# Two groups of experts at 128 slots with split weights, two at 64 slots with raw fp32 weights in column halves

## The chip, the cores and the metric

The kernel runs on one core of a Trainium2 chip. The metric is the device time of one execution in microseconds (us); the median of several executions is compared.

Names of engines in all that follows: PE is TensorE (matmuls), DVE is VectorE, ACT is ScalarE, POOL is GpSimd, SP is SyncE, which here issues the transfers of weights. A piece is one transfer of weights from HBM into on-chip memory; here it is 1 MB (1024 KB, 1.0486 million bytes).

## What is computed

Two layers of a transformer block over 256 tokens and 256 context tokens of width 1024: four kinds of attention, a gated merge, and a mixture of experts. The last layer keeps only the 256 tokens. The change touches the mixture of experts of that last layer:

```python
def moe(tok, router_w, router_b, w1, w3, w2):          # tok: 256 x 1024 in the last layer
    scores = jax.nn.sigmoid(tok @ router_w)            # 16 experts in 4 groups of 4
    biased = scores + router_b
    group = argmax(sum of the 2 best of biased in each group)   # one group per token
    idx = the 2 best experts of that group
    wts = scores[idx] / sum(scores[idx])
    ...
    y_e = (silu(x @ w1[e]) * (x @ w3[e])) @ w2[e]      # w1, w3: 1024 x 512, w2: 512 x 1024
    out[token] = sum over its 2 experts of wts * y_e
```

All weights are fp32. Every one of the 16 experts is used by some token, so all 16 x 6 MB are read.

## The kernel before

TensorE's fast path here multiplies a reduced fp32 type (fp32r). To keep fp32 accuracy the kernel splits every operand into an exact high and low part and forms a product by three matmuls (`mm3`, L262: high x high, high x low, low x high; they are the rows L263, L264 and L265).

The last layer's experts. Each token chooses one group of four experts. The routing (L1543 to L1660) computes on chip, on small tables, which group a token takes and its rank in the group; group g owns the 128 slots from 128 g on, so 512 slots in all. A one-hot matrix `OH` [token, slot] (L1620) gathers the tokens into the slots by matmuls (L1633); the gathered tokens are scaled (`hf`, L1637), and split into the parts `xe`, which share the buffer `hT` (L1640, L1641). `group_tables` (L1706) gathers the weights of a slot (`wsl`) and the transposed one-hots `OHT`.

The loop over experts (L1731) goes through them in the order 0 to 15. Step i forms x @ w1 and x @ w3 of expert i (two times 8 x 3 matmuls of 128x512 into the banks `h1` and `h3`), `act_in` makes silu times product times slot weight, and then, for expert i - 1, four transposes (L258) and 4 x 2 x 3 matmuls with w2 into two banks that collect the four experts of a group. After a group's last expert the sum is split (`y_parts`, L1467) and goes back to the tokens by matmuls with `OHT` (`combine`, L1480, L1486), which adds to the residual `xt` (L1495). At step 1 `overflow` (L1499) reads the largest count of a group (`mxi`, a number in a register of every engine), and a branch (L1504) runs a second, general pass over all experts for tokens beyond the 128 slots.

The weights. The class `Stream` (L93) holds the pieces in the order of use. `issue` (L117) starts transfers from SP while fewer than `cap` buffers are in use (7 for the experts, set at L1728); a transfer is one row L131. `_split` (L137) makes the parts: ACT copies to the high part `whi` (L285), DVE subtracts to get the low part `wlo` (L289), each sixth time POOL instead (L287). A raw buffer is free when all of its 512-column quarters are split. Four pairs of `whi` and `wlo` exist. The order of everything on an engine is that in which the program issues it, as rearranged by the framework's scheduler.

What waits for what around the change: SP issues a piece when its buffer is free, so it stands behind the splits; ACT and DVE stand behind the landing of a piece and behind PE (a pair of parts must be used before it is overwritten); PE stands behind the splits.

Of the kernel before, what the change touches and what calls it, by code (L numbers as in the profile page):

```python
# [19 lines left out]
P = 128  # L20
# [3 lines left out]
NE = 16  # L24
# [9 lines left out]
# packed small parameters: name -> width  # L34
# [5 lines left out]
for _n, _w in SM:  # L40
# [4 lines left out]
# packed constants (shapes alone)  # L45
CS = [("ident", 128), ("natm", 64), ("cos", 64), ("sin", 64), ("cosm", 32), ("sinm", 32),
      ("iota", 128), ("encg", 4), ("pidx", 1), ("cv", 32), ("one", 1), ("sel", 32)]
# [8 lines left out]
def shape_constants():  # L56
# [23 lines left out]
    put("iota", j)  # L80
    put("encg", 4.0 - np.arange(4)[None, :])
# [11 lines left out]
class Stream:  # L93
    """Weights in the order of use: DMA ahead, then exact high and low parts ahead of TensorE."""
# [19 lines left out]
    def issue(self):  # L114
        while self.nd < min(len(self.pieces), self.lim) and (self.live < self.cap or self.spare):
# [11 lines left out]
            for (p0, p1, s) in pc["loads"]:  # L127
# [45 lines left out]

    def done(self, i):
        self.live -= 1


SP2, SP4, SPT = 1, 1, 1
ADA_ORDER = ((1, 0), (0, 1), (0, 2), (1, 1), (1, 2))
# [8 lines left out]
def kernel(ctx: ExitStack, tc: tile.TileContext, a, out, dbg=None, depth=L):  # L188
# [65 lines left out]
    def transposes(src, kts):  # L254
        """Transposes of 128-column blocks of src into one bank."""
# [5 lines left out]
    def mm3(o, s, whl, start, stop):  # L261
        """s = (high, low) stationary parts, whl = (high, low) moving parts."""  # L262
# [13 lines left out]
    # silu(c), silu(c_ctx): row k = p * KT + kt of ada_w  # L276
# [32 lines left out]
    def plan_ada0():  # L309
        """The first modulation by columns: scale and shift of two blocks of d at a time."""  # L310
# [5 lines left out]
    def plan_in0():  # L316
        """Keys, values and queries of the window heads by rows, as h comes first."""
# [36 lines left out]
    def plan_out(l):  # L354
        """w_out by halves of its columns, for one pair of tiles of tokens after the other."""
# [23 lines left out]

    for l in range(depth):  # L380
# [14 lines left out]
        plan_out(l)  # L395
        for i in range(NE + 1):
# [53 lines left out]
    def ada_bias(l, r):  # L450
        """ada_b, and for the last round the second norm's gain, laid out as the products."""
# [41 lines left out]
    # biases of the first modulation (shift, scale) and the first norms' gains, d on partitions  # L493
# [12 lines left out]
    def ada0(c):  # L506
        """Scale and shift of blocks 2c and 2c + 1 of d; four column groups hold parts of the sum."""
# [92 lines left out]
    def rope_tables(T):  # L600
        """Gains times the rotations' cosines and sines; the router's tables share their place."""
# [19 lines left out]
    def attention_layer(l, T, hT):  # L621
# [24 lines left out]
        def norm_heads(x, H, hd, ct, stt, rot0):  # L646
            """x [P, H, hd] in SBUF, in place: rms over hd, gain and rotation."""
# [35 lines left out]
        def qk_post(nats, tiles, H, gname, dst, lo=None):  # L683
# [6 lines left out]
            def p2(t):  # L690
# [5 lines left out]
                else:  # L696
                    # of each head the high part on its own rows, the low part on those of the other
# [36 lines left out]
        def std_slots(operands, vsel, yT, pairs, sink=False, bias=None, mask=False):  # L734
            """Slots of work: P V of one pair of heads, scores of the next unit, transposes of the one before."""
# [114 lines left out]
        def heads(q, k):  # L850
            """Products of a pair of heads: the high part of the queries with both parts of the keys, then the low one."""
# [10 lines left out]
        def stage_win():  # L862
# [14 lines left out]
            def kv(t):  # L877
                """By tiles of tokens: h comes so from the layer before."""
# [246 lines left out]
    def steps0(ev_kv, ev_q):  # L1125
        """The first projections, block by block of d as the modulation arrives."""
# [39 lines left out]
    for l in range(depth):  # L1166
# [10 lines left out]
        def run_ada(steps, stage):  # L1177
            """With the rounds of the modulation that go with this stage."""
# [65 lines left out]
        wm.lim = E_IDS[l, NE - 1, 2][-1][-1][0] + 1  # L1244
# [34 lines left out]
        # router weights with the second norm's gain, and what its shift adds to the logits  # L1279
# [15 lines left out]
        def finish(t, j, ps):  # L1295
            """Half of the columns of a tile of x; its part of the logits."""
# [74 lines left out]
        if nT > 2:  # L1371
            norms()
        if not last:
# [543 lines left out]
```

## Time and profile before

| | us |
|---|---|
| runs | 2021.88, 2022.29, 2023.82 |
| median | 2022.29 |
| the profiled execution: its span, and with what lies around it | 2020.5, about 2022.3 |
| last layer's experts, first to last matmul of their loop | 1711.8 to 2010.4 |

| engine | busy us | share of the span |
|---|---|---|
| PE | 1902.2 | 94% |
| DVE | 1456.5 | 72% |
| ACT | 1255.0 | 62% |
| POOL | 812.2 | 40% |

The span is the time from the first to the last instruction of the profiled execution; 1.8 us lie around it up to the median of the runs. A matmul of the fast type is one record in the timeline; a raw fp32 matmul of 256 or 512 columns is two, so x8 of such a row are four matmuls. "Granted clock" is the share of full speed that TensorE's throttle gave. "DMA share" is the mean busy share of the 16 transfer engines of the core.

### The profile page before, as it was taken

How to read it: one execution, taken by the hardware profiler on the slowest of the kernel's cores; microseconds unless marked ns; L12 is line 12 of the kernel's file. 1: busy time of each engine (PE TensorE's matmuls, PEld its weight loads, DVE VectorE, ACT ScalarE, POOL GpSimd, SP SyncE). 2: the span in 40 equal slices, each digit the busy share in tenths (PEclk: the TensorE clock that was granted, in tenths of full speed). 3: DMA queues.
4: the chain of work that ended last, by engine and by line, in shares of the span. 5: the costliest groups of instructions: out<-in, count | busy, mean ns of one | idle time of the engine just before them, and what ended most of it. 6: DMA issues, size and time to landing. Idle time of an engine off the chain costs nothing. (4 is left out here: it accounts for less than half of the span.)

```text
span 2020.5 us, 28368 instructions
## 1 busy us (share of the span) xinstructions
PE 1902.2 (94%) x9124; PEld 1412.6 (70%) x9124; DVE 1456.5 (72%) x2614; ACT 1255.0 (62%) x2605; POOL 812.2 (40%) x1126
## 2 busy tenths in 40 slices
PE   7989999999999999599999979999999998999998
PEld 5746678776666677377777766667777676777776
DVE  4657465657556546788888976865767776999998
ACT  4436465455435435389999855554656555889887
POOL 0657353536346400544433326641446511323231
PEclk9989999999999999699999988999999998999999
DMA  9340242211662347689999572355322473899995
GB/s 337 123 139 29 76 136 71 63 42 41 261 231 63 106 137 260 231 290 358 361 357 352 201 265 88 147 198 167 105 92 62 125 273 124 293 342 355 335 331 198
DMA packets 174145, 392.23 MB, mean 194 GB/s; under 512 B 13089, under 2 KB 30785, under 8 KB 168864
## 3 DMA queue, kind: packets, MB, share of 16 engines
q1 hardware_dynamic: 167200, 377.29, 53.9%
q0 software_dynamic: 4320, 7.94, 1.1%
q10 hardware_dynamic: 2464, 5.08, 0.7%
q8 instruction: 75, 1.23, 0.3%
q14 instruction: 86, 0.70, 0.1%
HBM read 381.21 MB, written 16.84 MB: 197 GB/s over the span
## 5 line engine op out<-in xcount | busy, mean ns | idle before, releaser
L285 ACT ACTIVATE whi<-raw 128x512 fp32r<-128x512 f32 x608 | 374.5, 631 | 61.9 <-PE h L265 34.8
L289 DVE TENSOR_TENSOR wlo<-raw,whi 128x512 fp32r<-128x512 f32 x509 | 378.1, 791 | 41.1 <-ACT whi L285 40.5
L251 ACT ACTIVATE whi<-raw 128x512 fp32r<-128x512 f32 (+1 forms) x376 | 231.7, 625 | 251.2 <-PE acc L265 188.3
L264 PE MATMUL acc<-wlo,hT 128*128 128x512 f32 (+2 forms) x976 | 385.0, 394 | 0.2 <-DVE wlo L252 0.2
L265 PE MATMUL acc<-whi,hT 128*128 128x512 f32 (+2 forms) x976 | 379.1, 390 | 0.2 <-DVE hT L252 0.2
L252 DVE TENSOR_TENSOR wlo<-raw,whi 128x512 fp32r<-128x512 f32 (+1 forms) x376 | 278.3, 751 | 136.1 <-ACT whi L251 134.8
L263 PE MATMUL acc<-whi,hT 128*128 128x512 f32 (+2 forms) x976 | 363.9, 398 | 2.9 <-ACT nat L955 1.1
L287 POOL TENSOR_TENSOR wlo<-raw,whi 128x512 fp32r<-128x512 f32 x99 | 140.0, 1414 | 295.4 <-ACT whi L285 270.9
L263 PEld LDWEIGHTS acc<-whi,hT 128*128 128x128 f32 x976 | 182.6, 189 | 55.7 <-issue 11.1
L264 PEld LDWEIGHTS acc<-wlo,hT 128*128 128x128 f32 x976 | 184.1, 189 | 44.2 <-issue 8.5
L265 PEld LDWEIGHTS acc<-whi,hT 128*128 128x128 f32 x976 | 183.8, 188 | 39.3 <-issue 5.8
L238 POOL TENSOR_SCALAR pp<-pp,sml 128x512 f32<-128x512 f32 (+1 forms) x168 | 119.4, 720 | 143.3 <-DVE sml L731 92.9
L726 ACT ACTIVATE pp<-S,sml 128x512 f32<-128x512 f32 (+1 forms) x192 | 117.2, 612 | 86.1 <-DVE sml L721 58.3
L721 DVE TENSOR_REDUCE sml<-S 128x1 f32<-128x512 f32 (+1 forms) x192 | 112.8, 596 | 43.7 <-PE S L712 42.2
L558 POOL TENSOR_TENSOR sml<-sml,nhalf 128x1 f32<-128x1 f32 (+3 forms) x110 | 121.2, 1104 | 7.0
L557 POOL TENSOR_SCALAR sml<-sml 128x1 f32<-128x1 f32 (+3 forms) x110 | 38.5, 350 | 191.1 <-DVE sml L652 114.2
L264 PE MATMUL h<-wlo,hT 128*128 128x512 f32 x256 | 105.0, 410 | 6.2 <-DVE wlo L289 5.8
L264 PE MATMUL h<-wlo,xe 128*128 128x512 f32 x256 | 105.5, 412 | 5.2 <-POOL wlo L287 4.0
L289 DVE TENSOR_TENSOR wlo<-w,whi 128x512 fp32r<-128x512 f32 x139 | 99.6, 760 | 11.7 <-ACT whi L285 11.7
L258 PE MATMUL T<-cst,pp 128*128 128x128 f32 x560 | 91.2, 286 | 12.9 <-POOL pp L238 9.3
L264 PE MATMUL S<-wlo,yh 128*128 128x512 f32 x256 | 103.1, 403 | 0.0
L285 ACT ACTIVATE whi<-w 128x512 fp32r<-128x512 f32 x160 | 96.8, 630 | 9.5 <-PE S L265 2.5
(383 smaller groups left out, 3900.8 us busy)
## 6 DMA issues: line engine op xcount, KB each, us to landing
raw<-in_moe_w_dram SPq DMA_DIRECT2D x152, 1024.0 KB
raw<-in_w_in_dram SPq DMA_DIRECT2D x124, 512.0 KB
raw<-in_ada_w_dram SPq DMA_DIRECT2D x48, 1024.0 KB
w<-in_moe_w_dram SPq DMA_DIRECT2D x16, 1024.0 KB
w<-in_moe_w_dram SPq DMA_DIRECT2D x64, 256.0 KB
raw<-in_w_branch_dram SPq DMA_DIRECT2D x24, 512.0 KB
raw<-in_w_out_dram SPq DMA_DIRECT2D x24, 512.0 KB
w<-in_moe_w_dram SPq DMA_DIRECT2D x16, 512.0 KB
```

The costliest lines, as they stand in the source:

```text
L238: G.tensor_scalar(o, i, s, s2, op0=OP.mult, op1=OP.mult)
L251: act(hi, src, AF.Copy)
L252: V.tensor_tensor(lo, src, hi, op=OP.subtract)
L263: mm(o, s[0], whl[0], start=start, stop=False)
L264: mm(o, s[0], whl[1], start=False, stop=False)
L265: mm(o, s[1], whl[0], start=False, stop=stop)
L285: act(hi, raw, AF.Copy)
L287: G.tensor_tensor(lo, raw, hi, op=OP.subtract)
L289: V.tensor_tensor(lo, raw, hi, op=OP.subtract)
L558: G.tensor_tensor(r, r, nhalf[:, :n], op=OP.pow)
L721: V.tensor_reduce(nm[:, i:i + 1], ps[i][:, :nk], axis=AX.X, op=OP.max, negate=True)
L726: act(p[:, :nk], ps[i][:, :nk], AF.Exp, bias=nm[:, i:i + 1], accum_out=nm[:, 2 + i:3 + i])
```

## The change

The diff does six things in the last layer.

1. The groups are ordered on chip by the number of their tokens (`key`, `pos`, L1705 to L1708 of the new program). Group 0 always takes place 0; the other three follow by count, the largest first. A place q has the number of its group in `gid[q]`, a register of SP for places 1 to 3 (`values_load`, L1732).
2. Places 0 and 1 keep 128 slots and the three fast matmuls. Places 2 and 3 get 64 slots each.
3. For places 2 and 3 the weights are not split: PE multiplies the raw fp32 buffer by the gathered fp32 tokens `xh`, 64 rows of the stationary operand's columns at a time, two matmuls at once in the two column halves of the array (`tile_position=(0, 0)` and `(0, 64)`): x @ w3 in one half and x @ w1 in the other (`half_in`, L1870), and the two halves of w2's columns (L1915).
4. The 16 steps follow the fixed order `SEQ` of (place, expert in the group), in which full and half places alternate from the third step on.
5. The pieces of places 1 to 3 are loaded by an address known at run time (`bass.ds(gid[q], 1)`). Only the 10 pieces that belong to place 0 or come before the first of another place may be issued ahead of the routing (`wm.lim = LAST0[0]`). The one part of `hT` that is free now (tag hT1) gives two more buffers, named `w_17920` in the rows below, so nine in all.
6. Overflow now begins at 128 tokens in places 0 and 1 and at 64 in places 2 and 3.

The core of the diff:

```diff
+HALF = 64
+SEQ = ((0, 0), (0, 1), (2, 0), (0, 2), (2, 1), (0, 3), (2, 2), (1, 0), (2, 3), (1, 1), (3, 0), (1, 2), (3, 1), (1, 3), (3, 2), (3, 3))
...
+    def plan_place(l, i, which):
+        q, u = SEQ[i]
...
+        w = a[("moe_w1", "moe_w3", "moe_w2")[which]][l].rearrange("(g u) d f -> u g d f", u=4)[u]
+        kts, n = (4, 512) if which < 2 else (2, 1024)
+        def load(k0):
+            e = slice(0, 1) if q == 0 else bass.ds(gid[q], 1)
+            return [(0, P, w[e, k0 * P:(k0 + kts) * P, :].rearrange("o (k p) n -> p (o k) n", p=P))]
+        def piece(k0):
+            if q and not LAST0:
+                LAST0.append(len(wm.pieces))
...
-        wm.lim = E_IDS[l, NE - 1, 2][-1][-1][0] + 1
+        wm.lim = LAST0[0] if last else E_IDS[l, NE - 1, 2][-1][-1][0] + 1
...
+            totals(gsel, 4)
             rank = ranks(gsel, 4)
+            V.scalar_tensor_tensor(key, rk[:, 256:260], 4.0, C("encg"), op0=OP.mult, op1=OP.add)
+            V.memset(key[:, 0:1], BIG)
+            V.tensor_tensor(pc4[:, 0], key[:, None, :].to_broadcast([P, 4, 4]), key[:, :, None].to_broadcast([P, 4, 4]), op=OP.is_gt)
+            V.tensor_reduce(pos, pc4[:, 0], axis=AX.X, op=OP.add)
...
+            for q in range(1, 4):
+                gid[q] = nc.values_load(gxi[0:1, q:q + 1], engines=(mybir.EngineType.SP,), min_val=0, max_val=3)
+            wm.lim = len(wm.pieces)
+            wm.issue()
...
-                hf = t2("hf")
+                hf = t2("hf")[:, 0:256]
-                    act(hf, pt, AF.Identity, scale=A_, bias=B_)
+                    act(hf, pt[:, 0:256], AF.Identity, scale=A_, bias=B_)
...
+                xo_, xi_ = xh[:, k].rearrange("p (g s) -> p g s", g=2), pt[:, 256:512].rearrange("p (g s) -> p g s", g=2)[:, :, 0:64]
+                if k % 2:
+                    act(xo_, xi_, AF.Identity, scale=A_, bias=B_)
...
+            def half_in(i):
+                q, u = SEQ[i]
+                hh, x = banks["hh"], slice((q - 2) * 64, (q - 1) * 64)
+                for k in range(KT):
+                    for which, r in ((1, 0), (0, 64)):
+                        pi, kk = E_IDS[l, i, which][k]
+                        mm(hh[r:r + 64], xh[:, k, x], wm.cols(pi, kk * 512, 512), start=k == 0, stop=k == KT - 1, tile_position=(0, r))
+                        if kk == 3:
+                            wm.done(pi)
...
+                act(s1[0:64], hh[64:P], AF.Silu)
+                V.scalar_tensor_tensor(s1[0:64], s1[0:64], wsl[0:64, 4 * q + u:4 * q + u + 1], hh[0:64], op0=OP.mult, op1=OP.mult)
...
+            def out_of(i):
...
+                        if q < 2:
+                            mm3(py[q][j], (aT[i][0][:, k], aT[i][1][:, k]), wm.hl(pi, kk), u == 0 and k == 0, u == 3 and k == 3)
+                        else:
+                            mm(py[q][j * 64:j * 64 + 64], aT[i][:, k * 64:(k + 1) * 64], wm.cols(pi, kk * 512, 512),
+                               start=u == 0 and k == 0, stop=u == 3 and k == 3, tile_position=(0, 64 * j))
...
+            for i in range(NE + 1):
+                if i == 1:
+                    overflow()
```

How the change moves instructions, first on SP, between the output projection's weights and the branch of `overflow` (mxi is the largest count, gxi the table of group numbers). Before:

```order
L131 DMA raw<-in_w_out_dram 128x2x512 x4
L131 DMA raw<-in_moe_w_dram 128x4x512
L1268 DMA g_17938<-mod_71 128x1024
L131 DMA raw<-in_moe_w_dram 128x2x1024 x2
L131 DMA raw<-in_moe_w_dram 128x4x512
L1503 TENSOR_LOAD mxi
L1503 ISA x2
L1504 COMPARE_AND_BRANCH
```

The same place of SP in the changed program:

```order
L132 DMA raw<-in_w_out_dram 128x2x512 x4
L132 DMA w_17920<-in_moe_w_dram 128x4x512
L132 DMA w_17920<-in_moe_w_dram 128x2x1024
L132 DMA raw<-in_moe_w_dram 128x2x1024
L1331 DMA g_17941<-mod_71 128x1024
...
L132 DMA raw<-in_moe_w_dram 128x4x512
L1587 TENSOR_LOAD mxi
L1587 ISA x2
L1588 COMPARE_AND_BRANCH
```

Where "..." stands SP loads gxi three times (L1732) and issues two pieces by a run-time address; with the one after it that makes three such pieces. 13 pieces are issued before the branch and 83 after it.

On DVE, between the choice of the group (`gsel`) and the one-hots (`OH`), before:

```order
L1586 TENSOR_TENSOR gsel<-cst,t_17964 128x8
L1616 TENSOR_SCALAR rkm<-gsel 128x8
L1646 SCALAR_TENSOR_TENSOR M<-cn,gsel 128x32
L1646 SCALAR_TENSOR_TENSOR oh<-cn,gsel 128x32 x2
L1617 TENSOR_TENSOR rkm<-rkm,rk 128x8
L1693 TENSOR_TENSOR wd<-sc,M 128x32
L1666 TENSOR_TENSOR mv<-oh,cst 128x96 x2
L1620 TENSOR_TENSOR OH<-cst,rkm 128x512 x2
```

Now 35 small operations stand in that place instead of 8. The chain that leads to `OH` among them:

```order
L1670 TENSOR_TENSOR gsel<-cst,t_17967 128x8
...
L1705 SCALAR_TENSOR_TENSOR key<-rk,cst 128x4
...
L1707 TENSOR_TENSOR pc_17987<-key 128x16
...
L1708 TENSOR_REDUCE pos<-pc_17987 128x4
...
L1712 TENSOR_TENSOR rkm<-gsel,pos 128x8
...
L1714 TENSOR_REDUCE tpos<-rkm 128x2
...
L1717 TENSOR_TENSOR rkm<-cst,tpos 128x8
...
L1718 TENSOR_SCALAR rkm<-rkm 128x8
...
L1719 TENSOR_TENSOR rkm<-rkm,gpos 128x8
...
L1723 TENSOR_TENSOR OH<-cst,rkm 128x256 x4
```

On PE, one half step amid the full ones in the changed program (yh is the bank of a half place's w2, hh that of its w1 and w3, S_ the banks of a full place's w2, h_ the bank of a full place's w1 or w3):

```order
L1915 MATMUL yh<-raw,aTh 64x512 x4
L277 MATMUL h_18158<-whi,xe 128x512
L278 MATMUL h_18158<-wlo,xe 128x512
L279 MATMUL h_18158<-whi,xe 128x512
L272 MATMUL T<-cst,s_19780 128x128 x4
L1870 MATMUL hh<-raw,xh 64x512 x16
L277 MATMUL S_19847<-whi,yh 128x512
```

There 16 matmuls in column halves stand in one block between full ones, where the program before has 48 matmuls of 128x512.

## Rows read from the trace of the kernel before

**Rows 1.** The page: span, and busy time of each engine (share) xinstructions.
```profile
span 2020.5 us, 28368 instructions
PE 1902.2 (94%) x9124; PEld 1412.6 (70%) x9124; DVE 1456.5 (72%) x2614; ACT 1255.0 (62%) x2605; POOL 812.2 (40%) x1126
```

**Rows 2.** Busy time by stretch: whole expert stage, then three stretches in it.
```profile
core 0: us, PE busy (x) PEld busy (x) DVE busy (x) ACT busy (x) POOL busy (x), PEclk, DMA share, GB/s
1711.80:2010.40 298.60, 292.27 (x1273) 226.23 (x1273) 277.24 (x387) 258.20 (x429) 89.23 (x63) 1.00 0.87 310
1750.00:1790.00 40.00, 40.00 (x175) 31.08 (x174) 36.27 (x51) 36.38 (x61) 13.14 (x10) 1.00 1.04 392
1820.00:1870.00 50.00, 50.00 (x218) 39.20 (x217) 45.17 (x63) 45.44 (x75) 15.64 (x12) 1.00 0.99 354
1900.00:1950.00 50.00, 49.68 (x218) 38.55 (x217) 45.65 (x65) 45.23 (x76) 15.89 (x11) 1.00 1.01 355
```

**Rows 3.** The chain that ended last: start us, us, engine, line.
```profile
2010.11 0.24 PE S L265
2010.37 0.70 DVE yg L1473
...
2016.21 0.59 DVEq L1913
```

**Rows 4.** The transfers of pieces; what SP waited for: us, times, longest.
```profile
L131 SPq DMA_DIRECT2D raw<-in_moe_w_dram x96: 367/368/930, 1623.6 to 1989.7; - x96
SPq L131 <- DVE wlo L289: 270.6, 88, 27.5
```

**Rows 5.** Lines by form in the expert stage: the splits of the pieces, the transposes.
```profile
L289 DVE TENSOR_TENSOR wlo<-raw,whi 128x512 fp32r<-128x512 f32 x321 | 237.4, 791 | 19.1 <-ACT whi L285 18.4
L285 ACT ACTIVATE whi<-raw 128x512 fp32r<-128x512 f32 x380 | 234.8, 630 | 36.4 <-PE h L265 21.1 <-PE S L265 0.7 <-ACTq L1504 0.3
L258 PE MATMUL T<-cst,s 128*128 128x128 f32 x64 | 9.8, 273 | 0.0
```

**Rows 6.** PE's timeline, the modulation's matmuls: four column groups of 32, raw fp32.
```profile
107.22 1.07 PE L478 MATMUL S<-raw,cs 128*32 128x512 f32 x8
109.11 2.78 PE L478 MATMUL S<-raw,cs 128*32 128x512 f32 x24
117.50 1.92 PE L478 MATMUL S<-raw,cs 128*32 128x512 f32 x16
```

**Rows 7.** PE's timeline, an attention product in column halves of 64, fp32.
```profile
1638.10 1.95 PE L766 MATMUL T<-pT,nV 128*64 128x256 f32 x16
```

**Rows 8.** PE's timeline, four column groups of 32 amid full matmuls.
```profile
562.07 0.40 PE L263 MATMUL acc<-whi,hT 128*128 128x512 f32 x1
562.40 1.07 PE L478 MATMUL S<-raw,cs 128*32 128x512 f32 x8
563.39 0.51 PE L264 MATMUL acc<-wlo,hT 128*128 128x512 f32 x1
563.73 0.40 PE L265 MATMUL acc<-whi,hT 128*128 128x512 f32 x1
```

**Rows 9.** The routing: DVE's timeline, PE's clock, the first copy of gathered tokens.
```profile
1703.22 0.17 DVE L1586 TENSOR_TENSOR gsel<-cst,t 128x8 bf16<-128x8 f32 x1
1703.42 0.17 DVE L1616 TENSOR_SCALAR rkm<-gsel 128x8 f32<-128x8 bf16 x1
1704.32 1.28 DVE L1620 TENSOR_TENSOR OH<-cst,rkm 128x512 fp32r<-128x512 f32 x2
1700.00:1710.00 10.00, 5.13 (x20) 4.16 (x20) 6.75 (x39) 2.78 (x6) 0.00 (x0) 0.59 0.01 2
1709.61 0.78 ACT L1637 ACTIVATE hf<-pt,B,A 128x512 f32<-128x512 f32 x1 [5.98 <-PE pt L1633]
```

**Rows 10.** SP's timeline, the last piece before the branch and the first ones after it.
```profile
1728.13 0.37 SPq L131 DMA_DIRECT2D raw<-in_moe_w_dram  x1
1735.95 2.27 SPq L131 DMA_DIRECT2D raw<-in_moe_w_dram  x3
```

More of the change, by code (lines that the diff above doesn't have):

```diff
@@ L126, in issue @@
             n = min(k * w, self.width // len(tiles))
-            for (p0, p1, s) in pc["loads"]:
+            for (p0, p1, s) in (pc["loads"]() if callable(pc["loads"]) else pc["loads"]):
                 for c in range(0, k * w, n):
@@ L172, in raw, with cols @@
         return self.pieces[i]["raw"][0]
+    def cols(self, i, c, n):
+        self.issue()
+        tiles = self.pieces[i]["raw"]
+        w = self.width // len(tiles)
+        return tiles[c // w][:, c % w:c % w + n]
     def done(self, i):
-        self.live -= 1
+        if self.pieces[i]["own"]:
+            self.live -= 1
+        else:
+            self.spare.append(self.pieces[i]["raw"])
 SP2, SP4, SPT = 1, 1, 1
+HALF = 64
+SEQ = ((0, 0), (0, 1), (2, 0), (0, 2), (2, 1), (0, 3), (2, 2), (1, 0), (2, 3), (1, 1), (3, 0), (1, 2), (3, 1), (1, 3), (3, 2), (3, 3))
 ADA_ORDER = ((1, 0), (0, 1), (0, 2), (1, 1), (1, 2))
@@ L378, in plan_expert, with plan_places @@
                 ids += [[(i, 0), (i, 1)], [(i, 2), (i, 3)]]
+    gid, LAST0 = {}, []
+    def plan_place(l, i, which):
+        q, u = SEQ[i]
+        ids = E_IDS.setdefault((l, i, which), [])
+        w = a[("moe_w1", "moe_w3", "moe_w2")[which]][l].rearrange("(g u) d f -> u g d f", u=4)[u]
[6 more added lines that the diff above has]
+                LAST0.append(len(wm.pieces))
+            i = wm.add(lambda: load(k0), kts, n, split=False)
+            if q < 2:
+                pc = wm.pieces[i]
+                if which < 2:
+                    pc.update(g=1, s0=len(wm.sub))
+                else:
+                    pc.update(kts=4, w=512, left=4, g=1, s0=len(wm.sub), rows=2)
+                for s in range(4):
+                    wm.sub.append((i, s))
+            return i
+        for k0 in range(0, KT if which < 2 else 4, kts):
+            yield
+            i = piece(k0)
+            if which < 2:
+                ids += [(i, k) for k in range(4)]
+            else:
+                ids += [[(i, 0), (i, 1)], [(i, 2), (i, 3)]]
+        yield
+    def plan_places(l):
+        for i in range(NE + 1):
+            if i < NE:
+                g1, g3 = plan_place(l, i, 0), plan_place(l, i, 1)
+                order = [g1, g1, g1, g3, g3, g3] if SEQ[i][0] < 2 else [g1, g3] * 3
+                for g in order:
+                    next(g)
+            if i >= 1:
+                for _ in plan_place(l, i - 1, 2):
+                    pass
     for l in range(depth):
@@ L1476, in y_parts, with y_half, combine_last @@
             return r
+        def y_half(py):
+            hi, lo = (gp.tile([P, 512], F32R, name="yp", tag="t2", bufs=BUFS["t2"]) for _ in range(2))
+            y = t2("yg")
+            for j in range(2):
+                r = slice(j * 64, j * 64 + 64)
+                V.tensor_tensor(y[r], py[r], g2[0][r, j * 512:(j + 1) * 512], op=OP.mult)
+            parts(hi, lo, y)
+            return [[(v[j * 64:(j + 1) * 64]) for v in (hi, lo)] for j in range(2)]
+        def combine_last(t, q, yp, j):
+            ps = psT()
+            r = slice(0, P) if q < 2 else slice(j * 64, j * 64 + 64)
+            for i in range(2):
+                mm(ps, OHT[q][r, t * P:(t + 1) * P], yp[j][i], start=i == 0, stop=i == 1)
+            cs = slice(j * 512, (j + 1) * 512)
+            V.tensor_tensor(xt[t][:, cs], xt[t][:, cs], ps, op=OP.add)
         def combine(t, terms, js=range(2)):
@@ L1499, in overflow @@
         def overflow():
[L1501 removed]
+            nmax = nT * P + (HALF if last else 0)
+            nblk = -(-nmax // CAP)
             if nblk > 1:
[L1503 removed]
+                mxr = nc.values_load(mxi[0:1, 0:1], min_val=0, max_val=nmax)
                 with tc.If(mxr > CAP):
@@ L1625 @@
+            wm.issue()
+            V.tensor_scalar(gix, pos, 2.0, float(CAP - HALF), op0=OP.is_ge, op1=OP.mult)
+            V.tensor_tensor(gix, gix, rk[:, 256:260], op=OP.add)
+            V.tensor_reduce(mx[:, 0:1], gix, axis=AX.X, op=OP.max)
+            V.tensor_copy(mxi, mx[:, 0:1])
         if not last:
@@ L1737 @@
+        for i in range(0 if last else NE + 1):
             if i == 14 and not last:
```

123 lines of the change are left out of this document (99 added, 24 removed).

## The prediction

> **What bounds the kernel now.** I read the page first: PE is busy 1902.2 of 2020.5 us [rows 1], so a change that takes work from PE can pay, if it does so in a stretch where PE is the limit. The change touches the last layer's experts alone, so I next read the busy times of that stage [rows 2]. It lasts 298.6 us, PE works in 292.27 of them, at the full granted clock. Inside, PE has no gap: 40.00 of 40.00 and 50.00 of 50.00 us. DVE and ACT are close behind (277.24 and 258.20 us), and the transfers are not far either: 310 GB/s on average, 392 GB/s in the stretch 1750 to 1790. The chain of waits [rows 3] shows the end: the last matmul with w2 starts at 2010.11, then the sum is split, sent back to the tokens and stored. From 2010.4 to the end of the span, 10.1 us, nothing else runs. Of the waits, SP's own [rows 4] matter: it waited 270.6 us in 88 times for the splits to free a buffer. So the transfers are held back by the buffers, which are held by the splits, which follow PE.
>
> One more reading decides later. In 1820 to 1870 and 1900 to 1950 the rate is only 354 and 355 GB/s at a DMA share near 1 [rows 2]. That can be a limit of the transfers, or only what PE asks for. An expert is 6 pieces, 6.29 MB; PE's 175 records in 40.00 us are 0.2286 us each, an expert has 72 matmuls and 4 transposes, so 17.4 us; 6.29 MB in 17.4 us is 362 GB/s. The 354 is thus about PE's own demand, and the 392 in the earlier stretch, where buffers were empty, is a rate that the transfers do reach.
>
> **The change part by part.** I work against the profiled execution, 2020.5 us of span; the median of the runs, 2022.29, lies 1.8 above it.
>
> *PE's work in half experts.* Eight of 16 experts stay at 17.4 us. A half expert has 16 + 8 matmuls in column halves, 12 pairs. No row shows a 512-column pair in halves of 64; two rows bound it. The modulation's matmuls go four at a time in column groups of 32, raw fp32, 512 columns [rows 6]: one set takes 1.07 us, two 1.92, three 2.78, so each further set costs 0.855. The attention product in halves of 64 [rows 7] has 8 matmuls of 256 columns, four pairs, in 1.95 us with its start: 0.49 per pair, 0.98 for 512 columns. I take 0.855, since the 0.98 contains a start-up that a block of eight pairs pays once: 12 x 0.855 = 10.3. The four transposes have half the columns of those at 0.273 us [rows 5]: 0.4 for all. The block is entered and left twice per expert; around a single set in column groups the starts are 0.33 and 0.34 us apart (562.07 to 562.40, 563.39 to 563.73 [rows 8]) where 0.23 is normal, so 0.1 each, 0.4 for four. Sum 11.1 us, 6.3 less than now; for eight, **-50.4 us**. By 0.98 it would be 12.6 and -38.
>
> The Trainium skill, TensorEngine Tiling (Array Packing), Key Properties, says that a change of the tiling mode drains TensorE. The 0.1 us at each border agrees, and a drain of that size does not change the sum.
>
> *Splits.* Half of them go: of 630 ns on ACT and 791 on DVE [rows 5]. They were hidden under PE; their going buys nothing by itself, but the raw buffer of a half place is now freed by PE's last matmul on it instead of a split.
>
> *Routing.* Between the group choice and the one-hots DVE has 35 small operations where it had 8. From 1703.42 to 1704.32 eight of them took 0.90 us, 0.11 each; the dependent step before it (1703.22 to 1703.42) 0.20 [rows 9]. So 27 more cost 3.0 to 5.4 us, I take 4. PE idles there: it is busy half of 1700 to 1710, so all of it is on the path. The gathered copies shrink from 512 columns (0.78 us the first [rows 9]) to 256 and 128 on two engines; I give back 1. Together **+3 us**.
>
> *SP.* Its three register loads and three run-time addresses come while it would wait for buffers anyway: before, between 1728.13 and 1735.95 it issued nothing [rows 10]. Zero; if that cover went, a few us of the start below.
>
> *Tail.* The last place's sum is one bank rather than two, the same four products to the tokens: zero, between -2 and +1.
>
> PE alone would so end at 2010.4 - 50.4 + 3 = 1963.0; with the tail 1973.1, a time of 1975.
>
> *Transfers.* They are not made fewer: 96 pieces before [rows 4], 96 now. A full and a half expert together are 12.58 MB in 17.4 + 11.1 = 28.5 us of PE: 441 GB/s asked for, more than the 392 that any of the stretches shows. So the transfers become the limit. By the order on SP 13 pieces are issued before the branch and 83 after it, 87.0 MB. The first issue after the branch stood at 1735.95 [rows 10]; with the routing 1739. The rate: at least 354, at most 392 [rows 2]. I take 380, near the upper, because the 354 was demand; and below it because in the first steps after the branch the nine buffers are full and free up at PE's pace. 87.0 MB / 380 GB/s = 229 us, to 1968. The last piece's two pairs 1.7, the tail 10.1: 1979.8 of span. Where PE (1973.1) and the transfers (1979.8) are so close, each at times waits for the other; I add 2 us, less than the 2.8 that one piece takes at 380 GB/s. Span 1982, **time 1984**: 38 us less than now; of the 50 that PE saves, 3 go to the routing and 9 to the transfers.
>
> **The rivals.**
>
> *PE stays the bound, 1975.* For it: nine buffers instead of seven, and 392 GB/s in 1750 to 1790 with splits still holding buffers. At 392 the 83 pieces take 222 us and end at 1961, before PE. Against: 392 stands in one stretch of 40 us only.
>
> *The transfers hold 354 GB/s, 2000.* If the 0.99 and 1.01 of DMA share beside 354 and 355 [rows 2] mean that engines were full, 87.0 MB take 245.8 us, to 1985; with 1.7, 10.1, 2 and 1.8 about 2000. Against: the share is 1.04 at 392, so a share of 1 does not tell a ceiling.
>
> The Trainium skill, HBM Reference, Specifications, gives some 358 GB/s as a core's effective share, and says that a core that streams alone measures about 425. By 358 the time would be 1998, by 425 PE would stay the bound; the 392 [rows 2] agrees with the second, as one core runs here.
>
> *The halves do not run side by side: slower, 2057.* If two matmuls in column halves of one bank went one after the other, a half expert would have 24 x 0.855 + 0.8 = 21.3 us, 3.9 more than a full one; eight of them +31, with the routing +3 and the rest as now: 2057. It decides from 1.35 us per pair on, where 12 pairs cost as much as is saved (12 x 1.35 + 0.8 = 17.0, and the 3 us of routing over eight experts 0.4). Against: four groups of 32 take 0.855 together, and pairs of 64 at most 0.98 per 512 columns [rows 6, 7]. For: in neither row are the two moving operands different weights that have just landed.
>
> *The change does not do what it says: the overflow pass runs, far slower.* With 64 slots in the smaller places, a place with over 64 tokens would send the kernel through the branch, and the pass reads all experts again, 100.7 MB: 257 us at 392 GB/s, so 2240 and more. The reference on its inputs sends 64, 97, 36 and 59 tokens to the groups; group 0 goes to place 0, the 97 to place 1, 59 and 36 to the halves, so nothing overflows, by a margin of five tokens.
>
> **How the numbers follow.** Chances: transfers at about 380 (1984) 0.50; PE bound (1975) 0.20; transfers near 354 (2000) 0.21; halves in sequence 0.04; overflow 0.01; 0.04 for what I have not seen, half of it slower. The range takes in the first three with their bounds. Its low end is the PE case with 392 throughout and less than 3 us of routing, 1970; its high end the 354 case and 5 us of routing, with pairs at more than 0.855 and thus some waits more, 2005. A measurement of this kernel tells 0.2%, about 4 us, from no change. Faster by more: the first three cases and part of the rest, 0.93; within: 0.02; slower: 0.05.
>
> **What would show it.** In the stage PE's share falls from 98% to near 95%, and its idle time is ended by landings (of raw buffers, or of splits that waited for one). The rate is 370 to 390 GB/s from the branch to the last piece. ACT's and DVE's split rows are halved in number. Pairs start 0.855 us apart in blocks of 16 matmuls; the first of a block comes 0.1 us late. SP's waits for buffers name PE's half matmuls beside the splits. The first gathered column comes 3 us later. The prediction is wrong if pairs are over 1 us apart, if the rate stays at 355 with several pieces under way, or if PE has no idle time in the stage; and the sum is wrong in a term if the stage's end moves by other than 40 us.

## The result and the profile after

| | before | changed |
|---|---|---|
| median of the runs, us | 2022.09 | 1991.69 (1989.69 to 1996.04) |
| ratio, 95% interval | | 0.9848 [0.9832, 0.9863] |
| span of the profiled execution | 2020.5 | 1990.3 |
| choice of the groups (`gsel` on DVE) | 1703.2 | 1708.1 |
| from that choice to the end of the span | 317.3 | 282.1 |

The kernel is about 30 us faster; 1984 was forecast, in a range of 1970 to 2005. From the choice of the groups on, where the change works, it is 35 us faster (33 to 36 with the repeats further down). The other 5 us are lost ahead of the choice, where next to nothing was changed; the last experiment comes back to that. All comparisons of profiles below are of the stretch from the choice to the end, called the stage.

The page of the changed kernel (span; busy time of the engines, share, instructions) and its busy time by stretch: the stage from 1717.5 on, then its long middle, then the beginning in pieces of 10 us, then the end, where the last bytes of weights arrive.

```profile
span 1990.3 us, 27486 instructions
PE 1866.3 (94%) x8932; PEld 1334.6 (67%) x8932; DVE 1337.7 (67%) x2471; ACT 1130.4 (57%) x2411; POOL 764.7 (38%) x1094
```

```profile
core 0: us, PE busy (x) PEld busy (x) DVE busy (x) ACT busy (x) POOL busy (x), PEclk, DMA share, GB/s
1717.50:1980.00 262.50, 251.25 (x1091) 146.07 (x1089) 158.99 (x228) 135.72 (x239) 41.17 (x31) 0.99 0.91 345
1770.00:1970.00 200.00, 193.80 (x824) 109.12 (x824) 121.41 (x167) 99.75 (x171) 31.96 (x24) 0.99 1.04 394
1740.00:1750.00 10.00, 7.20 (x36) 3.71 (x33) 2.71 (x4) 3.02 (x5) 1.30 (x1) 1.00 0.72 258
1750.00:1760.00 10.00, 9.85 (x43) 6.87 (x40) 6.55 (x9) 7.60 (x13) 2.67 (x2) 1.00 0.17 64
1760.00:1770.00 10.00, 10.00 (x48) 7.64 (x47) 9.32 (x13) 8.62 (x15) 2.60 (x2) 1.00 0.87 310
1970.00:1980.00 10.00, 9.81 (x48) 3.10 (x44) 1.31 (x3) 0.59 (x1) 0.00 (x0) 1.00 0.53 213
1976.00:1977.00 1.00, 1.00 (x6) 0.29 (x4) 0.00 (x0) 0.00 (x0) 0.00 (x0) 1.00 0.03 12
1977.00:1979.00 2.00, 2.00 (x12) 0.72 (x10) 0.00 (x0) 0.00 (x0) 0.00 (x0) 1.00 0.00 0
```

Against [rows 2]: DVE and ACT, which had been nearly full, are down to 61% and 52%. PE is still busy 193.80 of 200 us in the middle, and at the same time the transfers go at 394 GB/s without a pause, a rate that the kernel before reached in one stretch only. Two resources are nearly full at once. And there is a hole ahead of it: 64 GB/s from 1750 to 1760.

PE from its first to its last matmul with the experts' weights, in the kernel before and in the changed one:

```profile
1712.06:2010.81 298.75, 292.42 (x1273) 226.04 (x1271) 277.65 (x387) 257.94 (x429) 88.97 (x63) 1.00 0.87 310
1719.65:1979.82 260.17, 249.10 (x1081) 144.31 (x1079) 156.78 (x222) 133.60 (x233) 41.17 (x31) 0.99 0.92 348
```

PE has 43.3 us less to do, and it is idle 11.1 us where it was idle 6.3.

The hole is to be seen in SP's timeline (start, us, engine, line, operation), and in what SP (1725 to 1760) and PE (1700 to 1760) waited for:

```profile
1726.01 0.41 SPq L132 DMA_DIRECT2D raw<-in_moe_w_dram  x1
1731.21 3.57 SPq L132 DMA_DIRECT2D raw<-in_moe_w_dram  x2
1741.78 1.44 SPq L132 DMA_DIRECT2D raw<-in_moe_w_dram  x3
1758.77 3.97 SPq L132 DMA_DIRECT2D w<-in_moe_w_dram  x2
```

```profile
SPq L132 <- DVE wlo L303: 38.8, 5, 15.5
SPq L1588 <- SPq L1588: 5.5, 1, 5.5
```

```profile
PE hh L1870 <- DMA raw<-in_moe_w_dram: 4.5, 2, 2.6
```

Between the third and the fourth run-time piece stands the branch (L1588), 1734.8 to 1741.8. Then three pieces go out, and the next one not until 1758.77: it waits 15.5 us for a split to free its buffer. The half matmuls of step 2 (`hh`, L1870) meanwhile run ahead of the second full expert, on pieces that have only just been issued; PE waits 4.5 us for them, and the second full expert, whose splits free that buffer, comes later by their time. Whether that makes the hole is put to the test below.

The end answers to [rows 3]: the chain that ended last (start, us, engine, line), with the last matmuls and the first step of the sum behind them. From 1979.8 to the end of the span it is 10.5 us, 10.1 before.

```profile
1974.51 5.33 PE yh L1915 x24
...
1979.86 0.68 DVE yg L1549
```

The cost of the half matmuls is near the forecast. PE's timeline, one block of 16 matmuls with w1 and w3, one of four with w2 (eight records), the transposes; then, from a block whose two operands lie in differently named buffers, the single records:

```profile
1853.52 7.09 PE L1870 MATMUL hh<-raw,xh 128*64 128x512 f32 x32
1863.76 0.46 PE L1901 MATMUL T<-cst,s 64*128 64x64 f32 x4
1844.63 1.94 PE L1915 MATMUL yh<-raw,aTh 128*64 128x512 f32 x8
...
1963.54 0.59 PE L1870 MATMUL hh<-w,xh 128*64 128x512 f32 x1
1963.54 0.59 PE L1870 MATMUL hh<-raw,xh 128*64 128x512 f32 x1
1963.97 0.59 PE L1870 MATMUL hh<-w,xh 128*64 128x512 f32 x1
1963.97 0.59 PE L1870 MATMUL hh<-raw,xh 128*64 128x512 f32 x1
```

7.09 + 2 x 1.94 + 0.46 = 11.4 us for a half expert, against 17.4 for a full one. The two halves do run side by side: their records start in the same moment, 0.43 us after the pair before.

PE's clock was not full throughout this time, as it had been in the kernel before. Ten us of the middle, and in them one block of eight matmuls that took 5.35 us, where such blocks elsewhere take 3.65 (1968.75):

```profile
1880.00:1890.00 10.00, 8.43 (x31) 2.90 (x31) 4.77 (x7) 1.83 (x4) 0.00 (x0) 0.83 1.04 398
1885.93 5.35 PE L1870 MATMUL hh<-raw,xh 128*64 128x512 f32 x16
```

Just before, PE had waited 1.57 us for the sum of a finished place. For part of these 10 us the granted clock was the lower of its two levels (1.2 instead of 2.4 GHz), which cost this block about 1.7 us.

### The profile page after: what moved, and what is told of

Same layout as the page of the kernel before. It is cut to its first block, busy times and chain, and to the rows that moved or that the text cites. A ratio compares the mean times of both kernels' runs of the same rounds, so it can differ in the third digit from the quotient of the medians.

```text
span 1990.3 us, 27486 instructions
## 1 busy us (share of the span) xinstructions
PE 1866.3 (94%) x8932; PEld 1334.6 (67%) x8932; DVE 1337.7 (67%) x2471; ACT 1130.4 (57%) x2411; POOL 764.7 (38%) x1094
## 5 line engine op out<-in xcount | busy, mean ns | idle before, releaser
L303 DVE TENSOR_TENSOR wlo<-raw,whi 128x512 fp32r<-128x512 f32 x309 | 231.6, 794 | 62.1 <-ACT whi L299 61.8
L299 ACT ACTIVATE whi<-raw 128x512 fp32r<-128x512 f32 x372 | 226.4, 630 | 78.0 <-PE h L279 35.7
L277 PEld LDWEIGHTS acc<-whi,hT 128*128 128x128 f32 x976 | 182.9, 189 | 56.3 <-issue 11.5
L301 POOL TENSOR_TENSOR wlo<-raw,whi 128x512 fp32r<-128x512 f32 x63 | 86.1, 1367 | 270.0 <-ACT whi L299 213.4
L278 PE MATMUL h<-wlo,xe 128*128 128x512 f32 x384 | 158.4, 413 | 6.2 <-POOL wlo L301 4.0
L277 PE MATMUL h<-whi,xe 128*128 128x512 f32 x384 | 151.3, 396 | 0.2 <-PEq L1588 0.2
L279 PE MATMUL h<-whi,xe 128*128 128x512 f32 x384 | 151.3, 394 | 0.0
L303 DVE TENSOR_TENSOR wlo<-w,whi 128x512 fp32r<-128x512 f32 x175 | 127.3, 772 | 16.9 <-ACT whi L299 16.8
L299 ACT ACTIVATE whi<-w 128x512 fp32r<-128x512 f32 x204 | 123.4, 630 | 24.3 <-PE h L279 7.4
L278 PEld LDWEIGHTS h<-wlo,xe 128*128 128x128 f32 x384 | 72.5, 189 | 48.2 <-POOL wlo L301 18.8
```

What stands on the lines that cost most here:

```text
L277: mm(o, s[0], whl[0], start=start, stop=False)
L278: mm(o, s[0], whl[1], start=False, stop=False)
L279: mm(o, s[1], whl[0], start=False, stop=stop)
L299: act(hi, raw, AF.Copy)
L301: G.tensor_tensor(lo, raw, hi, op=OP.subtract)
L303: V.tensor_tensor(lo, raw, hi, op=OP.subtract)
```

## Experiments

Each was run in several executions except where said. The stage is read from the profiled execution (span less the start of the row `gsel`); it is one execution of each, and two of the same kernel (the last rows of the table) show that differences under 3 us in it say nothing.

| kernel | median us | stage us |
|---|---|---|
| before | 2022.09 | 317.3 |
| changed | 1991.69 | 282.1 |
| e1_two: 192 of PE's matmuls less, some 44 us | 1986.89 | 282.0 |
| e2_w1: 16 pieces less, some 42 us of transfer | 2006.44 | 299.7 |
| e10_both: both | 1958.27 | 252.3 |
| e4_pin: no half matmuls ahead of the second full expert | 1987.87 | 284.9 |
| e5_branch0: branch ahead of the first expert | 1988.89 | 283.8 |
| e6_nobranch: no overflow pass | 1988.11 | 279.1 |
| e3_static: group numbers as constants | 1989.65 | 283.4 |
| e7_seq: half steps from the second step on | 1994.08 | 285.7 |
| e8_full3: three full steps first | 1993.66 | 289.9 |
| e11_unpaired: column halves by fours | 2007.06 | 301.9 |
| r_after: the changed kernel again | 1993.37 | 284.8 |
| r_before: the kernel before again, one execution | 2022.88 | 317.7 |

**Which limit: PE's work or the transfers?**

```diff
+    def mm2(o, s, whl, start, stop):
+        mm(o, s[0], whl[0], start=start, stop=False)
+        mm(o, s[0], whl[1], start=False, stop=stop)
-                        mm3(h13[which], (xe[0][:, k, s], xe[1][:, k, s]), wm.hl(pi, kk), k == 0, k == KT - 1)
+                        mm2(h13[which], (xe[0][:, k, s], xe[1][:, k, s]), wm.hl(pi, kk), k == 0, k == KT - 1)
...
-                            mm3(py[q][j], (aT[i][0][:, k], aT[i][1][:, k]), ...)
+                            mm2(py[q][j], (aT[i][0][:, k], aT[i][1][:, k]), ...)
```

> Edit: in the full places the third of the three matmuls (low part of the stationary operand by the high part of the weights) is left out, so the low-order part of those products is not computed. PE loses 8 x 24 matmuls of 0.23 us, 44 us; the transfers are the same. Theory T (once started, the transfers run full, at 395 GB/s from 1768 to 1975 in the changed kernel, and their 83 pieces after the branch set the end): little is gained, only what a faster start gives, 1978 to 1988. Rival P (PE's work sets the end, the transfers ride along): 1945 to 1955. In between would mean that both limits lie close together.

The stage took 282.0 us, the same as with all matmuls. The stretch of 200 us in the middle, the last bytes of weights, and what PE waited for in the 200 us:

```profile
1763.00:1963.00 200.00, 175.01 (x678) 81.35 (x679) 123.98 (x165) 92.99 (x169) 34.13 (x24) 0.97 1.04 394
1968.00:1969.00 1.00, 1.00 (x8) 0.30 (x6) 0.00 (x0) 0.00 (x0) 0.00 (x0) 1.00 0.06 25
```

```profile
PE hh L1875 <- DMA raw<-in_moe_w_dram: 7.6, 5, 1.8
PE h L284 <- DVE wlo L308: 5.9, 6, 1.8
```

From its first to its last matmul with weights PE is busy 224 us, 25 less than in the changed kernel. It is idle 25 of the 200 us now and waits for landings and for splits of what has just landed; the transfers go on at 394 GB/s. The last weights come in the 269th us after the choice (1700.33), as in the changed kernel (1976 to 1977, choice at 1708.14). So the transfers alone hold the end where it is.

The counterpart takes transfers away and leaves PE's work:

```diff
+            if which == 1 and q >= 2:
+                continue
             i = piece(k0)
...
+        if which == 1 and q >= 2:
+            ids += E_IDS[l, i0, 0]
...
```

> Edit: a half expert multiplies w1 in both column halves, so w3 of the eight half experts is neither loaded nor used: 16 pieces fewer, 16.8 MB, 42 us of transfer at 395 GB/s, with the same matmuls. T: the transfers cease to bind and PE sets the end; PE's waits in the stage go, some 4.5 us for the first half expert and some 6.5 us after 1768, so 1976 to 1984. P: no change, 1989 to 1994. If the half matmuls themselves were what is slow, no change either.

It was slower than the changed kernel, by 17.6 us in the stage, which no theory had. The transfers are down to 303 GB/s, PE is busy nearly as before:

```profile
1770.00:1970.00 200.00, 190.99 (x758) 98.59 (x759) 107.87 (x145) 92.89 (x156) 30.30 (x23) 1.00 0.84 303
```

What changed beside the load is the order. The framework's scheduler now breaks the half matmuls up and puts them between the full ones. PE's timeline shows one half expert (other half experts and the changed kernel have one or two blocks there, like the x32 above), and the waits a new one:

```profile
1857.62 1.08 PE L1875 MATMUL hh<-raw,xh 128*64 128x512 f32 x4
1859.52 1.08 PE L1875 MATMUL hh<-raw,xh 128*64 128x512 f32 x4
1861.88 2.79 PE L1875 MATMUL hh<-raw,xh 128*64 128x512 f32 x10
1866.79 0.66 PE L272 MATMUL T<-cst,s 128*128 128x128 f32 x4 [1.22 <-DVE s L1510]
```

```profile
PE T L272 <- DVE s L1510: 5.0, 5, 1.2
```

Counted over the stage, half matmuls stand in 43 blocks (30 of w1 and 13 of w2), in the changed kernel in 26. A block of one pair (four records) takes 1.08 us where a pair in the block of eight above takes 7.09 / 8 = 0.89, and the first full matmul behind it starts late too (0.33 us after, as in [rows 8]); by these, entering and leaving a block cost an estimated 0.3 us together, 5 us for 17 more. The transposes that wait for DVE add 4 (5.0 against 0.8). PE from its first to its last matmul with weights:

```profile
1719.89:1998.14 278.25, 264.15 (x1081) 143.72 (x1079) 157.48 (x222) 135.19 (x233) 40.77 (x31) 1.00 0.74 265
```

PE was busy 15 us longer than in the changed kernel, with the same number of matmuls; the blocks explain some 5 of them, and the rest I have not taken apart. So this run is no test of the transfers alone: PE sets its end, but in another order of work.

So both cuts were put together:

> Edit: both of the first two cuts at once: two matmuls instead of three in the full places (the low-order part of their products is not computed), and w3 of the half places neither loaded nor used. Each cut alone left the stretch from the choice of the groups to the end at 282.0 (PE's cut) and 299.6 us (the transfers' cut, with the matmuls broken into many more pieces). Theory B (PE and the transfers are each full, so that neither cut alone can help): together the stretch falls by 25 to 40 us, to 242 to 257, time 1948 to 1965. Rival T (only the transfers bind, and the second cut lost its gain to something else that is still there): 270 to 282 us. Rival P: as e1_two showed nothing, it would again be 282 or more.

The stage took 252.3 us, 30 less, and the time 1958. Neither cut alone gained anything in the stage (0 and -17.6), the two together 30. Here the order stayed in long blocks (28), which is part of it. After the last weights have come PE still works for 20 us:

```profile
1927.00:1937.00 10.00, 10.00 (x45) 3.66 (x45) 4.30 (x8) 2.25 (x4) 0.00 (x0) 1.00 0.00 0
```

So with less of both it is PE that sets the end, and with less on PE alone the transfers do. In the changed kernel the two limits lie within 11 us of each other: that is all of PE's idle time there, and faster transfers alone could gain no more. A run that takes transfers away and keeps the order is missing.

**The hole at the start.** Three edits aim at it. First the bank of the half products, so that those of step 2 can't run ahead:

```diff
-                hh, x = banks["hh"], slice((q - 2) * 64, (q - 1) * 64)
+                hh, x = banks["h1" if i == 2 else "hh"], slice((q - 2) * 64, (q - 1) * 64)
```

> Edit: the first half expert collects in the bank of the full experts' w1 product instead of its own, so its matmuls can't be moved ahead of the second full expert, as they are in the changed kernel. T with the start as the weak place: there the early half matmuls wait for their pieces, the second full expert comes late, and SP waits 15.5 us for a buffer that its splits free while the transfer engines stand nearly still (64 GB/s from 1750 to 1760); without it the transfers get going earlier, by 8 to 14 us: 1978 to 1985. P: only PE's own 4.5 us of waiting go: 1987. If the start doesn't matter: no change, 1990 to 1993, or slower by the wait for the bank.

The stage took 284.9 us: no gain. The median, 1987.87, is what the second of the three expectations gave; but in the profiled execution the 5 us lie ahead of the choice, which came that much earlier than in the changed kernel. PE's wait for `hh` is gone, but PE now stands at the branch, and SP still waits long for a split (12.6 us). So the half matmuls ahead of their turn do not make the hole by themselves:

```profile
PE h L277 <- PEq L1588: 5.8, 1, 5.8
```

Then the branch itself, ahead of the first expert (`if i == 0` for `if i == 1`):

> Edit: the branch to the overflow pass stands ahead of the first expert instead of behind it. SP then waits for the count while the buffers are full anyway, and can issue pieces through the time in which it now stands before the branch (1734 to 1742). T: transfers start earlier by some 5 to 8 us, 1983 to 1987; the early half matmuls stay early or not as the scheduler chooses. P: no change, 1990 to 1993. If PE's own way through the branch is longer than its wait for the gathered tokens, 1993 to 1998.

283.8 us, no gain. SP no longer stands at the branch behind the first expert (it still waits 14.3 us for a split), but PE starts its first full matmul 17.9 us after the choice instead of 11.5, since the gathered tokens are there before the branch is through:

```profile
PE h L277 <- ACTq L1588: 3.9, 1, 3.9
```

And no branch at all (the call of `overflow` left out):

> Edit: the overflow pass and its branch are left out, so tokens beyond a group's slots would be lost (there are none on these inputs). The stretch from the choice of the groups to the end of the span took 282.1 us in the changed kernel, 317.2 before; the stages ahead of it differ by up to 8 us between executions of like code, so that stretch is what is compared. T (the transfers' start is the weak place): SP issues on from 1734 instead of standing at the branch until 1742, PE does not wait there; the stretch falls by 6 to 12 us, time 1980 to 1986. Rival (the start is limited by the buffers that PE frees, whatever SP does): 0 to 3 us, 1988 to 1992.

279.1 us, 3 less than the first execution of the changed kernel and 6 less than its repeat below. That lies between the two expectations, at the edge of what can be told apart. SP's timeline shows why it isn't more: it issues on until 1738, but the wait for a split is still there, until 1752.

```profile
1723.03 15.39 SPq L132 DMA_DIRECT2D raw<-in_moe_w_dram  x6
1752.27 3.98 SPq L132 DMA_DIRECT2D w<-in_moe_w_dram  x2
```

**The run-time addresses.**

```diff
-            e = slice(0, 1) if q == 0 else bass.ds(gid[q], 1)
+            e = slice(GRP[q], GRP[q] + 1)          # GRP = (0, 1, 3, 2)
...
-                gid[q] = nc.values_load(gxi[0:1, q:q + 1], engines=(mybir.EngineType.SP,), min_val=0, max_val=3)
...
-        wm.lim = LAST0[0] if last else ...
+        wm.lim = len(wm.pieces) if last else ...
```

> Edit: the numbers of the groups of places 1 to 3 are constants (1, 3, 2, right for these inputs) instead of registers, and no piece waits for the routing. T: the buffers are full by then, so the stretch to the end stays within 3 us of 282.1 and the time within 1987 to 1994. Rival (the run-time address costs: late issue of the first pieces of place 2, or slower issues): the stretch falls by 5 us or more, under 1987.

283.4 us: addresses known only on chip cost nothing that can be told here. By then the buffers are full and SP waits for them anyway (26.5 us the longest time in this run).

**The order of the steps.** Half steps from the second step on, and the other way round three full steps first:

```diff
-SEQ = ((0, 0), (0, 1), (2, 0), (0, 2), (2, 1), (0, 3), (2, 2), ...
+SEQ = ((0, 0), (2, 0), (0, 1), (2, 1), (0, 2), (2, 2), (0, 3), ...      # e7_seq
+SEQ = ((0, 0), (0, 1), (0, 2), (2, 0), (0, 3), (2, 1), (2, 2), ...      # e8_full3
```

> Edit: the order of steps begins with full, half, full, half. Only 4 pieces come ahead of the routing instead of 10, but the half steps, which free six buffers in 11 us of PE's time instead of 17, come earlier. T as 'buffers must be freed sooner': the transfers run full from about 25 us after the choice instead of 54; less the five pieces that are loaded later (13 us), the stretch to the end falls by 5 to 15 us, 1977 to 1987. Rival (what is not loaded ahead is lost): the stretch grows by 8 to 13 us, 1998 to 2005.

285.7 us: neither the gain nor the loss. The transfers do start early, and are no longer full throughout, at 372 GB/s from 1730 to 1970, while PE is about as busy as before (95% of the stretch, in 32 blocks of half matmuls instead of 26):

```profile
1730.00:1970.00 240.00, 228.66 (x970) 132.03 (x968) 145.29 (x201) 125.01 (x212) 39.06 (x30) 0.99 0.99 372
1970.00:1980.00 10.00, 9.29 (x46) 2.96 (x42) 1.83 (x3) 0.59 (x1) 0.00 (x0) 1.00 0.05 20
```

The hole is nearly gone here, and the end does not come earlier. That does not separate the two limits: six pieces more have to come after the choice, 16 us at 394 GB/s, and so the weights are through at about the same time as in the changed kernel, some 267 us after the choice (1970 less 1703.4), but for a last 0.2 MB.

> Edit: the order of steps begins with three full steps of place 0, so 16 pieces need no run-time address and no half matmuls stand ahead of the second full step. T: PE frees buffers there at one per 2.8 us, nearly the pace of the transfers, without the 15.5 us in which SP waited; the stretch falls by 4 to 10 us, 1981 to 1988. Rival (full steps free buffers too slowly, the half steps are missed early and crowd the end, where they need 567 GB/s): the stretch grows by 3 to 8 us, 1995 to 2000.

289.9 us, slower by 5 to 8, which is the size that the rival gave. Its reason does not hold: this order moves only the first two half steps back by one place each and leaves the end as it was. Most of PE's waiting from 1712 to 1960 is at the branch and for the pieces of the half steps:

```profile
PE h L277 <- PEq L1588: 5.6, 1, 5.6
PE hh L1870 <- DMA raw<-in_moe_w_dram: 2.4, 2, 1.3
PE hh L1870 <- DMA w<-in_moe_w_dram: 2.3, 1, 2.3
```

**What running side by side is worth.** Four matmuls of one column half, then four of the other:

```diff
-                for k in range(KT):
-                    for which, r in ((1, 0), (0, 64)):
+                for k0 in range(0, KT, 4):
+                    for which, r in ((1, 0), (0, 64)):
+                        for k in range(k0, k0 + 4):
...
```

> Edit: in a half place's w1 and w3 four matmuls of one column half follow each other, then four of the other, instead of alternating; the same matmuls, pieces and blocks. If neighbours run side by side only when they alternate, each of the 8 x 8 pairs costs 0.855 us more, 55 us of PE; since PE has little room left, the stretch grows by 45 to 55 us, to 327 to 337, over the 317.2 of the kernel before, time 2036 to 2047. Rival (matmuls of the two halves overlap in any order within what is queued): 282 to 290.

301.9 us, between the two. A block of 16 matmuls takes 8.97 us where it took 7.09; one after the other it would be an estimated 16 x 0.855 = 13.7:

```profile
1857.31 8.97 PE L1871 MATMUL hh<-raw,xh 128*64 128x512 f32 x32
```

So the halves overlap also when they don't alternate, but only in part; how, no row here shows. In the stage the edit costs 17 to 20 us, more than 8 x 1.9 = 15, and all of it is seen, since PE has little room.

**How far the profile repeats.** The changed kernel and the one before once more (the latter in a single execution):

> The changed kernel again, to see how far its stretch from the choice of the groups to the end (282.1 us) and the moment of that choice (1708.1) repeat. B: the stretch repeats within 1 us, and the choice comes anywhere between 1700 and 1708, as in the other kernels with like code ahead of it. Rival (the change itself makes the earlier stages 5 us later): the choice again near 1708.

> The kernel before again, for the same: the choice of the groups stood at 1703.2, the stretch from it to the end took 317.2 us. B: the stretch within 1 us of that, the choice between 1700 and 1708.

The choice of the groups came at 1708.10 and 1703.21, as in the first executions; the stage took 284.8 and 317.7 us. So the stage repeats within 3 us, not within 1. The choice 5 us later looked like a cost of the change, the rival of the expectation. But e4_pin has on every engine the same instructions in the same order up to the choice, and there it came at 1702.77; over all kernels of the table with the change it lies between 1700.05 and 1708.32. The rows of three of them:

```profile
1708.10 0.17 DVE L1670 TENSOR_TENSOR gsel<-cst,t 128x8 bf16<-128x8 f32 x1
```

```profile
1702.77 0.17 DVE L1670 TENSOR_TENSOR gsel<-cst,t 128x8 bf16<-128x8 f32 x1
```

```profile
1700.33 0.17 DVE L1675 TENSOR_TENSOR gsel<-cst,t 128x8 bf16<-128x8 f32 x1
```

(the changed kernel's repeat, e4_pin, e1_two). So the instructions don't make it. The close agreement of the repeat is in part chance, as its executions stood 2.9 us apart on the way (the same copy on DVE, L876, starts at 278.88 in one and at 275.96 in the other); why a like kernel differs by 5 us stays open. The medians of these kernels differ by as much, and for that reason the stages were compared.

No version here that computes the whole result and keeps the overflow pass beats the changed kernel by more than can be told apart.

## Why the prediction was right

*The bound before* [rows 2]: PE, in every stretch of the stage. The size of the gain fits that, 35 us in the stage for 43 us less of PE's work; no run tests it by itself.

*PE's half experts.* 11.1 us forecast, 11.4 measured. The value taken from the column groups of 32 [rows 6], 0.855 us per pair, is what a pair in halves of 64 takes inside a block (7.09 us for eight pairs with entry and exit); the upper bound from [rows 7] was too high. For a border between a block and full matmuls the forecast took 0.1 us from [rows 8]; a block of one pair takes 1.08 us instead of 0.86, which is 0.1 for each of its two borders. The Trainium skill's page TensorEngine Tiling (Array Packing) states in Key Properties that a change of the tiling mode drains TensorE. The trace agrees with a drain of that size.

*PE's saving* was smaller than forecast all the same: 43.3 us of busy time instead of 50.4. The half experts' own 11.4 instead of 11.1 is 2.6 of that. The forecast let the block be entered and left twice per half expert, 16 blocks at 0.2 us; there are 26, at an estimated 0.3 us, 8 us instead of 3. These two overlap in part, and the rest is not taken apart. It hardly shows in the time, as the transfers ended later still.

*Routing.* +3 forecast; the first full matmul comes 11.5 us after the choice instead of 8.9, +2.7.

*The transfers become the limit*, and *PE stays the bound*: given as two cases with 0.50 and 0.20. The first holds: e1_two shows that less work on PE gains nothing. Of the second it holds that PE is close behind, with 11 us of idle time; its time of 1975 does not. e10_both shows that less of both gains 30 us.

*The transfers' sum* came out within 4 us in the stage. It had the first issue behind the branch 36 us after the choice, then 229 us at 380 GB/s, then 13.8 us to the end of the span (1.7, 10.1 and the 2 for waits). The trace has them as 33.6 (1741.78), 234.4 (to 1976.2, 371 GB/s) and 14.1: -2 + 5 + 0 = +3, and the stage's gain is 35.2 us where the sum had 38.5. The mechanism was right, also in that the rate in the middle is higher (394 GB/s) and the first steps pull it down "because in the first steps after the branch the nine buffers are full and free up at PE's pace". What was mis-sized is the price of these first steps: at 394 the 87.0 MB would take 221 us, so they cost 13 us, where the step from 392 to 380 had allowed 7. That allowance was worked out from no row, so it is partly luck that it came so near, and partly that the branch was passed 2 us earlier. The end has its own shift: behind the last weights six pairs with w2 stand in one block, 5.33 us, of which 3.6 are left after the last byte, and not two pairs.

*The time* is 8 us above the forecast: these 3, and the 5 ahead of the choice, which the sum took from the profiled execution of the kernel before.

*The rival at 354 GB/s* is out: the rate in the middle is 394, and the rows at a DMA share near 1 with 354 were PE's demand, as argued. The Trainium skill's page HBM Reference (Specifications) gives some 358 GB/s as a core's share and about 425 for a core that streams alone. The trace lies between them: 394 over 200 us, 401 at most in 10 us of the changed kernel. *Halves one after the other* is out by the records that start together, and e11_unpaired shows what even partial loss of it costs. *Overflow* is out: nothing ran in the branch.

*What would show it*: PE's share in the stage was to fall to near 95%; it is 96% (249.10 of 260.17). PE's idle time was to be ended by landings; of the 11.1 us only the 4.5 at the start are. That sign was wrong, since PE itself was nearly full. And the full clock, which the sum took over from the kernel before, was not granted throughout (about 1.7 us).

## What to carry to other kernels

When a change takes work from the engine that bounds a stage, work out at once what the next resource needs in that time: here PE's saving of 43 us was worth 35, since the transfers of the same 96 pieces were only that far behind. Where two resources meet, an experiment on one of them need not show a gain; cut both together before you call either of them free. And look at the first pieces behind a barrier by themselves: buffers that were full and waited for their splits held the transfers for 15 us that no average shows. Neither the branch nor the work moved ahead of its turn made that hole by itself; taking one of them away left a wait of 12.6 to 14.3 us.

## What the runs showed that was not expected

Less to transfer made the changed kernel slower: with 16 pieces fewer the scheduler broke 26 blocks of half matmuls into 43, and the stage grew by 17.6 us. An experiment that changes loads also changes the order where a scheduler decides it, so the order has to be compared before the times are.

Matmuls in two column halves overlap without alternating: blocks of four and four took 8.97 us, alternating ones 7.09, where an estimated 13.7 would be without any overlap.

PE and the transfers can both be nearly full for 200 us: 97% busy beside 394 GB/s.
